# Layer 1's first key, value and query projection taken from the stream before its norm, with the norm applied afterwards

## The chip, the cores and the metric

One core of a Trainium2 chip runs the whole program as one launch. The metric is the device time of that launch in microseconds; the time before is the median of three runs. A profile of one further execution gives the instructions of each engine: TensorE (PE, with its weight loads as PEld), VectorE (DVE), ScalarE (ACT), GpSimd (POOL) and SyncE (SP), whose queue issues the DMAs of this kernel. Times inside the execution are counted from the start of its span.

## What is computed

A backbone of two layers over 512 latent tokens and 256 context tokens of width 2048. The part that matters here is the entry of layer 1, the odd one:

```python
mod = silu_c @ w_mod[l] + b_mod[l]
shift, scale, gate = jnp.split(mod[:, None, :], 3, axis=-1)
...
h = rmsnorm(x, norm_g[l]) * (1.0 + scale) + shift
hc = rmsnorm(cx, norm_g[l]) * (1.0 + cscale) + cshift
...
u = h @ o_w_in[i]
uc = hc @ o_w_in[i]
```

`rmsnorm` divides each token by the root of the mean square over its 2048 values. From `u` come the heads of two attentions (C with 8 query heads on 2 key heads, D with low-rank queries and keys) and a gate. Layer 0 has the same frame with two other attentions.

## The kernel before

All activations lie transposed: 128 channels of the model on the partitions, the 768 tokens (512 latent, 256 context) along the free axis, so the stream is 16 chunks of 128x768. A matrix product of full precision is made of three products in float32r: an operand is split into a high part (ScalarE's cast, `wh`, `h`) and the rest (VectorE's subtraction, `wl`, `l`), and TensorE adds high by high, high by low and low by high (`mm_step`, L277 to L287). Weights come in blocks of 128 output columns; four chunks' worth of a block is one 128x512 tile that is loaded (`wraw`, L274), cast (L265) and subtracted (L224). There are four `wh` and four `wl` buffers and three `wraw` buffers.

Layer 0 ends with 16 output chunks (`out_chunk`, L683). Each adds the gated product to the old stream, stores the new one (`x1d`, L689), squares it on ScalarE (L695) and sums the squares over the chunks on GpSimd (`acc1`, L700), multiplies it on VectorE by `ascale`, which is (1 + scale) times the norm's gain (L697), and stores that to `xad` (L698).

Layer 1 starts at L724. `rstd_cols` (L244) sums the squares over the partitions on TensorE by a product with ones (L249), takes the root on ScalarE (L253) and the reciprocal on VectorE (L254). `spread` (L232) lays the result over all partitions with six small products (L229) and two copies out of PSUM (L236) into the tile `rs1`, 128x768. Then a loop over the 16 chunks k (L731 to L738) loads `xad[k]` (`xk`, L733) and makes the normed input with `make_h` (L351): `xn = xk * rs1` (L353, on VectorE for every third chunk and on GpSimd for the other ten), `h = xn + shift` rounded on ScalarE in two halves (L358), `l = (xn + shift) - h` on VectorE in two halves (L364). The h and l of all 16 chunks stay in 32 buffers, which the products of layer 0's end give free. In the same loop chunk k is multiplied into three accumulators at once (`odd_ps`): the first key block C_K0, the first value block C_V0 (512 latent and 256 context columns each) and the first query block C_Q0 (512 columns). After the loop the key is squared, normed and rotated (L799 to L815), the value is transposed (L816, with L481), the query is treated likewise (L821 to L829), attention starts, and projections of other blocks (`proj`, gates first) fill TensorE meanwhile.

In the background, `mod_later` (L165) computes the modulation for later use: it loads `mraw` (L172) and adds it up in `macc` on VectorE (L179); for layer 1's output gates it is let go only after the last `xk` load (`last_x`).

The order of the work on each engine is set when the program is built, by a scheduler that works on a timeline of its own; the queues then run strictly in that order. That holds for SyncE's queue too: a load that waits for a buffer holds up every DMA behind it.

Of the kernel before, what the change touches and what calls it, by code (L numbers as in the profile page):

```python
# [17 lines left out]
P = 128  # L18
# [23 lines left out]
def trunk_kernel(ctx: ExitStack, tc: tile.TileContext, T):  # L42
# [20 lines left out]
        return pss.tile([P, 1024], F32, tag="S", name="S")  # L63

    def slot(name):
        return sp["s3"].tile([P, TOK], F32, tag="s3", name=name)

    def slotr(name):
        return sp["s3"].tile([P, TOK], F32R, tag="s3", name=name)

    def oslot(name):
        return sp["s3"].tile([P, TOK], F32, tag="o", name=name, bufs=2)
# [156 lines left out]
            nc.tensor.matmul(dst[:, P * i:P * i + P], lhsT=cols[:, 2 * t:2 * t + 1].broadcast_to([P, P]), rhs=ident,  # L229
                             start=True, stop=True)  # L230

    def spread(cols, dst):  # L232
        for ts in ((0, 1, 2, 3), (4, 5)):
            tp = psj.tile([P, 512], F32, name="J")
            spread_to(tp, cols, ts)
            nc.vector.tensor_copy(dst[:, P * ts[0]:P * ts[-1] + P], tp[:, :P * len(ts)])  # L236

# [6 lines left out]
    def rstd_cols(accs, ts, dim, name, bank=jbank):  # L244

        mp = bank()
        steps = [(a, t) for a in accs for t in ts]
        for i, (a, t) in enumerate(steps):
            nc.tensor.matmul(mp[:, 2 * t:2 * t + 2], lhsT=a[:, P * t:P * t + P], rhs=ones[:, 0:2],  # L249
                             start=(i == 0), stop=(i == len(steps) - 1))  # L250
        rs = sm.tile([P, 12], F32, name=name, bufs=2)
        n = 2 * len(ts)
        nc.scalar.activation(rs[:, :n], mp[:, :n], AF.Sqrt, bias=epsc, scale=1.0 / dim)  # L253
        nc.vector.reciprocal(rs[:, :n], rs[:, :n])  # L254
        return rs
# [178 lines left out]
    def etile(name):  # L434
        return sp["ep"].tile([P, TOK], F32, tag="e", name=name)
# [281 lines left out]
    for j in range(NCH):  # L717
# [4 lines left out]


    w = T["ow"]  # L724
    rs1 = etile("rs1")
    spread(rstd_cols((acc1, sq), range(6), D_MODEL, "rsx"), rs1)
    s_start = sbanks()
    odd_cols = (C_K0, C_V0, C_Q0)
    odd_ps = [(psj.tile([P, 512], F32, name="J"), s_start[:, 256 * i:256 * i + 256] if i < 2 else None)
              for i in range(3)]  # L730
    for k in range(NCH):  # L731
        xk = slot("xk")
        last_x = nc.sync.dma_start(xk, xad[k])  # L733
        hT[k] = make_h(1, k, xk, rs1, tmp("xn"), "mod")
        for i, (lat, cx) in enumerate(odd_ps):
            if k % 4 == 0:
                ws4[i] = wsplit(wraw(w, odd_cols[i], k, 4), 4)
            mm_step(lat, cx, ws4[i][k % 4], hT[k], k == 0, k == NCH - 1, opens=(i % 2 == 0), closes=(i % 2 == 1))  # L738

    def scaled(cols, f):  # L740
        nc.vector.tensor_scalar(cols[:, :8], cols[:, :8], f, None, op0=ALU.mult)
# [329 lines left out]
```

## Time and profile before

| | |
|---|---|
| runs before | 2518.85, 2517.13, 2510.58 us; median 2517.13 us |
| the profiled execution | 2515.64 us, of which the span is 2513.9 us |
| mean granted TensorE clock | 0.985 of full speed |
| busy in the span | PE 2408.1 us, DVE 1570.2 us, ACT 1011.7 us, POOL 247.8 us |
| last product of layer 0's output chunks starts | about 1550 us |
| first product of layer 1's loop starts | 1560.08 us |
| last product of that loop starts | 1619.33 us |
| first product of the gate projection behind it | 1628.68 us |

In a row of the timeline the first number is the start, the second the duration; in brackets stands how long the engine sat idle before it and what ended that. An engine's next instruction can start a little before the one ahead is marked as ended, so the distance from start to start is the better price where rows follow closely. In a row of grouped instructions the total and the mean stand behind the bar, then the idle time before them.

### The profile page before, as it was taken

What the parts mean: (1) busy time and instruction counts of PE and PEld (TensorE: products, weight loads), DVE (VectorE), ACT (ScalarE), POOL (GpSimd) and SP (SyncE); (2) the same over time, 40 slices, a digit from 0 to 9 for tenths busy, and PEclk for the clock granted to TensorE, in tenths of its full rate; (3) what the DMA queues carried; (4) which work ended last, traced back from release to release, by engine and by line L of the source; (5) the groups of instructions that cost most, each with busy time, mean ns of one, the idle gap of its engine ahead of it and who ended that gap; (6) DMA issues with size and microseconds to landing.
All of it is one profiled execution on the core that took longest, in us unless ns stands there. A gap on an engine that the chain in (4) does not pass through costs nothing.

```text
span 2513.9 us, 36308 instructions
## 1 busy us (share of the span) xinstructions
PE 2408.1 (96%) x14234; PEld 2077.1 (83%) x14234; DVE 1570.2 (62%) x2796; ACT 1011.7 (40%) x1964; POOL 247.8 (10%) x160
## 2 busy tenths in 40 slices
PE   3898999999999999999989999899999999999998
PEld 1677888888888899989878888688888888888787
DVE  4358667556965787887566664757545336776534
ACT  3234555444454334323342222444434334554434
POOL 1111001001000011010001012200001010100010
PEclk8999999999999999999999999899999999999999
DMA  8853111111312343443325545425422221222234
GB/s 305 302 179 100 43 57 56 50 57 57 109 58 72 100 144 113 142 164 111 134 96 199 188 170 184 146 92 191 150 72 84 69 95 56 64 93 68 97 118 151
DMA packets 97931, 297.48 MB, mean 118 GB/s; under 512 B 11488, under 2 KB 12512, under 8 KB 97760
## 3 DMA queue, kind: packets, MB, share of 16 engines
q1 hardware_dynamic: 97760, 295.16, 34.7%
q8 instruction: 112, 1.84, 0.3%
q14 instruction: 59, 0.48, 0.1%
HBM read 269.16 MB, written 25.95 MB: 117 GB/s over the span
## 4 chain that ended last, share of the span: by engine, by line
PE 87%; DVE 6%; DMA 3%; issue 2%; ACT 1%; SPq 0%; ACTq 0%; DVEq 0%
PE J L284 22%; PE J L287 22%; PE J L285 22%; PE O L563 6%; PE S L505 4%; PE T L548 3%; PE S L501 3%; DMA mraw<-in_wm_dram 2%; PE T L151 1%; DVE macc L179 1%; DVE l L364 1%; PE J L187 1%; DVE wl L224 1%; PE T L249 1%; PE T L229 1%
## 5 line engine op out<-in xcount | busy, mean ns | idle before, releaser
L284 PE MATMUL J<-h,wh 128*128 128x512 f32 (+1 forms) x2224 | 789.0, 356 | 9.3 <-DVE sg L493 3.2
L285 PE MATMUL J<-l,wh 128*128 128x512 f32 (+1 forms) x2224 | 762.5, 353 | 3.6 <-DVE l L364 3.6
L287 PE MATMUL J<-h,wl 128*128 128x512 f32 (+1 forms) x2224 | 704.3, 355 | 9.2 <-DVE wl L224 9.2
L265 ACT CAST wh<-wraw 128x512 fp32r<-128x512 f32 x492 | 304.1, 620 | 682.1 <-PE J L285 581.3
L224 DVE TENSOR_TENSOR wl<-wraw,wh 128x512 fp32r<-128x512 f32 x500 | 363.7, 731 | 317.7 <-ACT wh L265 307.1
L284 PEld LDWEIGHTS J<-h,wh 128*128 128x128 f32 x2224 | 421.3, 189 | 94.3 <-issue 8.2
L285 PEld LDWEIGHTS J<-l,wh 128*128 128x128 f32 x2224 | 421.9, 190 | 56.7 <-DVE l L364 4.8
L287 PEld LDWEIGHTS J<-h,wl 128*128 128x128 f32 x2224 | 386.4, 190 | 44.1 <-DVE wl L224 12.4
L179 DVE SCALAR_TENSOR_TENSOR macc<-mraw,silc,macc 128x512 f32<-128x512 f32 x420 | 317.2, 787 | 34.6 <-DMA mraw<-in_wm_dram 31.9
L284 PE MATMUL J<-yh,wh 128*128 128x512 f32 (+1 forms) x800 | 275.3, 351 | 4.7 <-ACT yh L469 4.7
L285 PE MATMUL J<-yl,wh 128*128 128x512 f32 (+1 forms) x800 | 271.7, 350 | 1.0 <-DVE yl L224 0.9
L287 PE MATMUL J<-yh,wl 128*128 128x512 f32 (+1 forms) x800 | 253.6, 349 | 0.2 <-DVE wl L224 0.2
L517 DVE TENSOR_REDUCE nb<-S 128x1 f32<-128x768 f32 (+3 forms) x208 | 166.2, 799 | 140.0 <-PE S L505 73.0
L552 ACT CAST pth<-T 128x256 fp32r<-128x256 f32 (+2 forms) x288 | 125.0, 450 | 190.4 <-PE T L548 186.6
L284 PEld LDWEIGHTS J<-yh,wh 128*128 128x128 f32 x800 | 149.9, 189 | 31.6 <-ACT yh L469 5.5
L224 DVE TENSOR_TENSOR ptl<-T,pth 128x256 fp32r<-128x256 f32 (+2 forms) x288 | 144.2, 514 | 49.1 <-ACT pth L552 47.3
L285 PEld LDWEIGHTS J<-yl,wh 128*128 128x128 f32 x800 | 150.5, 189 | 22.3 <-DVE yl L224 3.1
L524 ACT ACTIVATE e<-S,nb 128x256 f32<-128x256 f32 (+3 forms) x144 | 104.3, 724 | 156.4 <-DVE nb L517 90.5
L287 PEld LDWEIGHTS J<-yh,wl 128*128 128x128 f32 x800 | 140.4, 189 | 13.2 <-DVE wl L224 0.5
L431 POOL TENSOR_TENSOR r<-r,cos 128x512 f32<-128x512 f32 x31 | 44.3, 1428 | 792.1 <-DVE t L430 736.2
L548 PE MATMUL T<-identr,e 128*128 128x128 f32 x784 | 116.3, 275 | 2.9 <-DVE e L534 2.6
L548 PEld LDWEIGHTS T<-identr,e 128*128 128x128 f32 x784 | 95.2, 142 | 16.7 <-issue 2.8
(283 smaller groups left out, 3143.7 us busy)
## 6 DMA issues: line engine op xcount, KB each, us to landing
mraw<-in_wm_dram SPq DMA_DIRECT2D x128, 512.0 KB, 3.7
wraw<-in_ew_dram SPq DMA_DIRECT2D x102, 512.0 KB, 3.7
wraw<-in_ow_dram SPq DMA_DIRECT2D x64, 512.0 KB, 3.6
wraw<-in_wo_dram SPq DMA_DIRECT2D x62, 512.0 KB, 3.8
mraw<-in_wm_dram SPq DMA_DIRECT2D x80, 384.0 KB, 7.4
xT<-in_xT_dram SPq DMA_DIRECT2D x16, 384.0 KB, 7.6
res<-in_xT_dram SPq DMA_DIRECT2D x16, 384.0 KB, 4.3
xad<-nx SPq DMA_DIRECT2D x16, 384.0 KB, 2.7
```

What stands on the lines that cost most here:

```text
L179: nc.vector.scalar_tensor_tensor(macc[:, v, :], rv[:, i, :], sc, macc[:, v, :], op0=ALU.mult, op1=ALU.add)
L224: nc.vector.tensor_tensor(o, a, h.bitcast(F32), op=ALU.subtract)
L265: nc.scalar.copy(wh[:, :n, :], rv[:, k0:k0 + n, :])
L284: nc.tensor.matmul(o, lhsT=wh, rhs=xh[:, c0:c1], start=first and (opens or o is lat), stop=False)
L285: nc.tensor.matmul(o, lhsT=wh, rhs=xl[:, c0:c1], start=False, stop=False)
L287: nc.tensor.matmul(o, lhsT=wl, rhs=xh[:, c0:c1], start=False, stop=last and (closes or o is lat))
L505: nc.tensor.matmul(S[:, 512:end], lhsT=q, rhs=k[:, 128 * lo:128 * hi], start=(i == 0), stop=(i == n - 1 and not masks))
L517: nc.vector.tensor_reduce(nb, S, axis=AX.X, op=ALU.max, negate=True)
L524: nc.scalar.activation(e, S, AF.Exp, bias=nb, scale=1.0 if scale is None else scale, accum_out=den)
L548: nc.tensor.transpose(out=tp[:, 128 * (b - b0):128 * (b - b0) + 128], in_=e[:, 128 * b:128 * b + 128], identity=ident)
L552: nc.scalar.copy(ph, tv)
L563: nc.tensor.matmul(o, lhsT=v[:, cols[i]], rhs=pt[part][:, i, :], start=(n == 0), stop=(n == len(steps) - 1))
```

## The change

The first loop no longer norms its input. It loads `xad[k]` into a tile of 770 columns, in two DMAs (512 latent columns, 256 context columns), and puts the two shift columns of the chunk (latent and context) between them. It casts and subtracts that tile (`xh`, `xl`, 770 columns wide) and multiplies it into the three blocks, so each accumulator holds the product of the weights with the scaled stream and, in two columns, with the shifts. The latent part takes 512 columns, the part behind it 258; the query block is cut in 256 and 258. `late_norm` then multiplies each accumulator by `rs1` on VectorE and adds the shift's product as a bias on ScalarE, into tiles in SBUF, which the code behind uses in place of the accumulators. `rs1` is now computed behind the loop in the code, with PSUM banks of another pool. A second loop loads every `xad[k]` again, into four buffers (two of tag `o`, two of tag `sg`), norms it in place and makes the h and l of all chunks for the other projections; it makes no product itself. `last_x`, for which the background waits, is now the last load of the first loop.

```diff
     rs1 = etile("rs1")
-    spread(rstd_cols((acc1, sq), range(6), D_MODEL, "rsx"), rs1)
     s_start = sbanks()
     odd_cols = (C_K0, C_V0, C_Q0)
-    odd_ps = [(psj.tile([P, 512], F32, name="J"), s_start[:, 256 * i:256 * i + 256] if i < 2 else None)
-              for i in range(3)]
+    first_ps = [jbank(), pso.tile([P, 512], F32, name="O"), jbank()]
+    q_bank = tbank()
     for k in range(NCH):
-        xk = slot("xk")
-        last_x = nc.sync.dma_start(xk, xad[k])
-        hT[k] = make_h(1, k, xk, rs1, tmp("xn"), "mod")
-        for i, (lat, cx) in enumerate(odd_ps):
+        xk = slot2("xk")
+        last_x = nc.sync.dma_start(xk[:, 0:512], xad[k][:, 0:512])
+        nc.sync.dma_start(xk[:, 514:770], xad[k][:, 512:768])
+        nc.vector.tensor_copy(xk[:, 512:514], modc[1][:, k, :])
+        xh, xl = slot2("xh", F32R), slot2("xl", F32R)
+        nc.scalar.copy(xh, xk)
+        sub(xl, xk, xh)
+        for i in range(3):
             if k % 4 == 0:
                 ws4[i] = wsplit(wraw(w, odd_cols[i], k, 4), 4)
-            mm_step(lat, cx, ws4[i][k % 4], hT[k], k == 0, k == NCH - 1, opens=(i % 2 == 0), closes=(i % 2 == 1))
+            wh, wl = ws4[i][k % 4]
+            if i < 2:
+                regs = ((first_ps[i], 0, 512), (s_start[:, 512 * i:512 * i + 258], 512, 770))
+            else:
+                regs = ((first_ps[i][:, 0:256], 0, 256), (q_bank[:, 0:258], 256, 514))
+            for n, (wk, xx) in enumerate(((wh, xh), (wh, xl), (wl, xh))):
+                for o, c0, c1 in regs:
+                    nc.tensor.matmul(o, lhsT=wk, rhs=xx[:, c0:c1], start=(k == 0 and n == 0),
+                                     stop=(k == NCH - 1 and n == 2))
+    spread(rstd_cols((acc1, sq), range(6), D_MODEL, "rsx", tbank), rs1, tbank)
+
+    def late_norm(name, parts, bias):
+
+        t = slot(name)
+        bc = sm.tile([P, 2], F32, name="bc", bufs=3)
+        nc.vector.tensor_copy(bc, bias)
+        for ps, c0, c1, v in parts:
+            nc.vector.tensor_tensor(t[:, c0:c1], ps, rs1[:, c0:c1], op=ALU.mult)
+            nc.scalar.activation(t[:, c0:c1], t[:, c0:c1], AF.Identity, bias=bc[:, v:v + 1])
+        return t
...
+    for k in range(NCH):
+        xk = (oslot, sgslot)[k % 2]("xk")
+        nc.sync.dma_start(xk, xad[k])
+        hT[k] = make_h(1, k, xk, rs1, xk, "mod")
```

The scheduler places the new instructions as follows. The first place is SyncE's queue where the loop's loads begin; `wraw` are the weights, `xad15` is layer 0's last store. Before:

```order
L274 DMA wraw_14984<-in_ow_dram 128x512
L733 DMA xk_14832<-xad0_109 128x768
L733 DMA xk_14875<-xad1_110 128x768
L689 DMA x1d15_108<-nx_14792 128x512
L733 DMA xk_14900<-xad2_111 128x768
L733 DMA xk_14925<-xad3_112 128x768
L733 DMA xk_14950<-xad4_113 128x768
```

Now, in the same place:

```order
L737 DMA xk_14807<-xad0_109 128x512
L738 DMA xk_14807<-xad0_109 128x256
L692 DMA x1d15_108<-nx_14792 128x512
L277 DMA wraw_15059<-in_ow_dram 128x512
L737 DMA xk_14851<-xad1_110 128x512
L701 DMA xad15_124<-nx_14792 128x768
L738 DMA xk_14851<-xad1_110 128x256
L737 DMA xk_14877<-xad2_111 128x512
L738 DMA xk_14877<-xad2_111 128x256
```

Half of chunk 1's load and all later ones now stand behind the store of `xad15`, which before stood behind the load of chunk 8.

The second place is VectorE's queue around the making of `rs1` (two copies out of PSUM); `xn` and the `xk` of L356 are the normed inputs, `l1_k` the low parts of the second loop, `xl` those of the first. Before:

```order
L254 RECIPROCAL rsx_14815<-rsx_14815 128x12
L697 TENSOR_SCALAR nx_14792<-nx_14792,modc1_194 128x512
L236 COPY rs1_14801<-J_14818 128x512
L236 COPY rs1_14801<-J_14824 128x256
L353 TENSOR_TENSOR xn_14834<-xk_14832,rs1_14801 128x768
L364 SCALAR_TENSOR_TENSOR l1_0_14837<-xn_14834,modc1_194,h1_0_14836 128x512
L364 SCALAR_TENSOR_TENSOR l1_0_14837<-xn_14834,modc1_194,h1_0_14836 128x256
L364 SCALAR_TENSOR_TENSOR l1_1_14880<-xn_14877,modc1_194,h1_1_14879 128x512
```

Now (`xl_14978` is chunk 5's, `xl_15030` chunk 7's):

```order
L227 TENSOR_TENSOR xl_14978<-xk_14973,xh_14977 128x770
L739 COPY xk_14999<-modc1_194 128x2
L227 TENSOR_TENSOR wl_15062<-wraw_15059,wh_15061 128x512
L239 COPY rs1_14801<-T_15311 128x512
L227 TENSOR_TENSOR xl_15004<-xk_14999,xh_15003 128x770
L739 COPY xk_15025<-modc1_194 128x2
L227 TENSOR_TENSOR xl_15030<-xk_15025,xh_15029 128x770
L739 COPY xk_15051<-modc1_194 128x2
L239 COPY rs1_14801<-T_15317 128x256
L356 TENSOR_TENSOR xk_15342<-xk_15342,rs1_14801 128x768
L356 TENSOR_TENSOR xk_15369<-xk_15369,rs1_14801 128x768
L227 TENSOR_TENSOR xl_15056<-xk_15051,xh_15055 128x770
```

The subtractions of chunks 0 to 7 stand ahead of the first normed input. From there on VectorE's queue mixes both loops: the subtraction of chunk 15 stands behind the `l` pair of chunk 14.

The third place is TensorE's queue where the small products of `spread` stand. Before, they are ahead of the loop's first product:

```order
L249 MATMUL J_14802<-ones_189,sq_14796 128x2 x6
L229 MATMUL J_14818<-identr_169,rsx_14815 128x128 x4
L229 MATMUL J_14824<-identr_169,rsx_14815 128x128 x2
L284 MATMUL J_14829<-h1_0_14836,wh_14844 128x512
L284 MATMUL J_14830<-h1_0_14836,wh_14856 128x512
```

Now the second copy's two stand in chunk 6 (`xh_15003`), and the first copy's four are spread over chunk 4:

```order
L753 MATMUL J_14803<-xh_15003,wh_14939 128x512
L753 MATMUL S_14802<-xh_15003,wh_14939 128x258
L753 MATMUL O_14804<-xh_15003,wh_14951 128x512
L753 MATMUL J_14805<-xh_15003,wh_14963 128x256
L753 MATMUL T_14806<-xh_15003,wh_14963 128x258
L232 MATMUL T_15317<-identr_169,rsx_15308 128x128 x2
L753 MATMUL J_14803<-xl_15004,wh_14939 128x512
```

Five chunks of products and the first five of chunk 6 now run ahead of the last small product.

More of the change, by code (lines that the diff above doesn't have):

```diff
@@ L65, in slot, with slot2 @@
     def slot(name):
-        return sp["s3"].tile([P, TOK], F32, tag="s3", name=name)
+        return sp["s3"].tile([P, TOK + 2], F32, tag="s3", name=name)[:, :TOK]
+    def slot2(name, dt=F32):
+        return sp["s3"].tile([P, TOK + 2], dt, tag="s3", name=name)
     def slotr(name):
-        return sp["s3"].tile([P, TOK], F32R, tag="s3", name=name)
+        return sp["s3"].tile([P, TOK + 2], F32R, tag="s3", name=name)[:, :TOK]
     def oslot(name):
@@ L230, in spread_to, with spread @@
                              start=True, stop=True)
-    def spread(cols, dst):
+    def spread(cols, dst, bank=None):
         for ts in ((0, 1, 2, 3), (4, 5)):
-            tp = psj.tile([P, 512], F32, name="J")
+            tp = (bank or jbank)()
             spread_to(tp, cols, ts)
@@ new lines, in trunk_kernel @@
+    spread(rstd_cols((acc1, sq), range(6), D_MODEL, "rsx", tbank), rs1, tbank)
[7 more added lines that the diff above has]
+        return t
+    odd_ps = []
+    for i in range(2):
+        cx = s_start[:, 512 * i:512 * i + 258]
+        t = late_norm("first", ((first_ps[i], 0, 512, 0), (cx[:, 2:258], 512, 768, 1)), cx[:, 0:2])
+        odd_ps.append((t[:, :512], t[:, 512:768]))
@@ L740, in scaled @@
+    t = late_norm("first", ((first_ps[2][:, 0:256], 0, 256, 0), (q_bank[:, 0:256], 256, 512, 0)), q_bank[:, 256:258])
+    odd_ps.append((t[:, :512], None))
+    for k in range(NCH):
+        xk = (oslot, sgslot)[k % 2]("xk")
+        nc.sync.dma_start(xk, xad[k])
+        hT[k] = make_h(1, k, xk, rs1, xk, "mod")
     def scaled(cols, f):
```

## The prediction

> **What bounds the kernel now.** I read the page first, then the busy time of the stretches around the change, then the groups and the timeline of the engine that is full there.
>
> ```profile
> span 2513.9 us, 36308 instructions
> ```
>
> The stretches (busy time of PE, PEld, DVE, ACT, POOL with counts, then clock, DMA share, GB/s) are cut at the start of the loop's first product, at the last `l`, at the loop's last product and at the first gate product:
>
> ```profile
> 1550.70:1560.08 9.38, 5.62 (x36) 5.16 (x35) 4.62 (x10) 2.15 (x5) 1.64 (x1) 0.82 0.96 318
> 1560.08:1602.94 42.86, 36.11 (x156) 28.27 (x157) 42.79 (x48) 20.78 (x38) 20.88 (x10) 0.84 0.47 169
> 1602.94:1619.56 16.62, 15.80 (x85) 13.27 (x85) 9.02 (x14) 4.52 (x9) 0.00 (x0) 1.00 0.83 259
> 1619.56:1628.68 9.12, 6.30 (x39) 5.73 (x38) 5.05 (x9) 3.27 (x9) 1.79 (x2) 0.81 0.54 181
> 1628.68:1700.00 71.32, 71.32 (x357) 60.46 (x358) 41.76 (x76) 33.30 (x58) 8.31 (x6) 0.98 0.26 90
> ```
>
> While the normed inputs are made, VectorE is busy 42.79 of 42.86 us: it sets the pace, not TensorE. Then TensorE catches up for 16.62 us, waits around the key's norm for 9.12 us, and is full afterwards. So what is lost before 1628.68 is lost for good. What VectorE did in its full stretch, by form:
>
> ```profile
> L364 DVE SCALAR_TENSOR_TENSOR l<-xn,modc,h 128x256 fp32r<-128x256 f32 x16 | 18.6, 1166 | 0.0
> L364 DVE SCALAR_TENSOR_TENSOR l<-xn,modc,h 128x512 fp32r<-128x512 f32 x16 | 15.7, 980 | 0.8 <-ACT h L358 0.8
> L353 DVE TENSOR_TENSOR xn<-xk,rs 128x768 f32<-128x768 f32 x5 | 4.7, 949 | 0.1
> L224 DVE TENSOR_TENSOR wl<-wraw,wh 128x512 fp32r<-128x512 f32 x6 | 4.0, 676 | 0.0
> L179 DVE SCALAR_TENSOR_TENSOR macc<-mraw,silc,macc 128x512 f32<-128x512 f32 x5 | 3.7, 738 | 0.0
> ```
>
> The narrow half of `l` takes longer than the wide one, which it should not. The timeline of VectorE at its undisturbed end gives the true prices, from start to start:
>
> ```profile
> 1596.95 0.94 DVE L353 TENSOR_TENSOR xn<-xk,rs 128x768 f32<-128x768 f32 x1
> 1597.82 0.47 DVE L364 SCALAR_TENSOR_TENSOR l<-xn,modc,h 128x256 fp32r<-128x256 f32 x1
> ...
> 1598.87 1.13 DVE L364 SCALAR_TENSOR_TENSOR l<-xn,modc,h 128x512 fp32r<-128x512 f32 x2
> 1599.93 1.28 DVE L224 TENSOR_TENSOR wl<-wraw,wh 128x512 fp32r<-128x512 f32 x2
> 1601.14 0.74 DVE L179 SCALAR_TENSOR_TENSOR macc<-mraw,silc,macc 128x512 f32<-128x512 f32 x1
> 1601.80 1.13 DVE L364 SCALAR_TENSOR_TENSOR l<-xn,modc,h 128x512 fp32r<-128x512 f32 x2
> ```
>
> An `xn` of 768 columns costs 0.87, an `l` pair 1.06, a `wl` 0.60, a `macc` step 0.66. By these, the stretch should hold 16 x 1.06 + 5 x 0.87 + 6 x 0.60 + 5 x 0.66 = 28.2 us; it took 42.8. The other 14.6 us are the ten norms on GpSimd, 1.46 each: a GpSimd row, then the VectorE row that began behind it.
>
> ```profile
> 1582.84 2.15 POOL L353 TENSOR_TENSOR xn<-xk,rs 128x768 f32<-128x768 f32 x1 [0.41 <-DVE l L364]
> ```
>
> ```profile
> 1583.23 2.69 DVE L364 SCALAR_TENSOR_TENSOR l<-xn,modc,h 128x512 fp32r<-128x512 f32 x2
> ```
>
> The pair took 2.69 instead of 1.13 us, since VectorE stood until GpSimd was done. The Trainium skill has the rule in "SBUF — State Buffer", section "Who interferes with whom": a VectorE instruction with two inputs in SBUF and a GpSimd one that reads SBUF shut each other out, and the second to come waits out the first. The trace agrees, with 2.69 us against 1.13.
>
> **The change, part by part.**
>
> *TensorE's work stays.* At full clock (a product's start, then the next block's):
>
> ```profile
> 1617.80 0.40 PE L284 MATMUL J<-h,wh 128*128 128x512 f32 x1
> ...
> 1618.85 0.40 PE L284 MATMUL J<-h,wh 128*128 128x512 f32 x1
> ...
> 1619.56 1.40 PE L249 MATMUL T<-ones,sq 128*128 128x2 f32 x12
> 1622.19 2.57 PE L229 MATMUL T<-identr,rsx 128*128 128x128 f32 x12 [1.23 <-DVE rsx L254]
> 1624.56 1.49 PE L481 MATMUL J<-identr,ev 128*128 128x128 f32 x6
> ...
> 1628.68 0.50 PE L284 MATMUL J<-h,wh 128*128 128x512 f32 x1 [0.84 <-ACT ev L825]
> ```
>
> A key or value step (2304 columns) takes 1.05 us, so 2.19 columns a nanosecond, and a query step 0.71. The two or three added columns and the cut query block change nothing by this rate: 2.81 us a chunk, 45 for all.
>
> *The start moves little.* ScalarE's queue has chunk 0's cast behind layer 0's last square:
>
> ```profile
> 1550.34 0.62 ACT L265 CAST wh<-wraw 128x512 fp32r<-128x512 f32 x1 [3.59 <-PE J L285]
> 1551.81 0.84 ACT L695 ACTIVATE sq<-nx 128x768 f32<-128x768 f32 x1 [0.85 <-DVE nx L688]
> ```
>
> With 0.9 for 770 columns (0.62 for 512) chunk 0 starts about 1553.5, without the norm. Chunk 1 cannot follow so soon.
>
> ```profile
> 1554.69 0.41 DVE L697 TENSOR_SCALAR nx<-nx,modc 128x512 f32<-128x512 f32 x1
> ```
>
> ```profile
> 1555.51 0.60 SPq L698 DMA_DIRECT2D xad<-nx  x1
> ```
>
> ```profile
> DMA to landing us min/median/max: 3.8/5.4/8.3
> ```
>
> Half of its load stands behind the store of `xad15`, which waits for that VectorE row. Even if the store goes 0.8 us sooner (the reciprocal no longer stands ahead), that half is issued about 1555 and lands at 1559 to 1560.5; with the cast, chunk 1 starts at about 1560, where before the whole loop started. The gain here is chunk 0's 2.8 us, and it only makes TensorE wait earlier.
>
> *`rs1` comes late.* Before, its second copy was here:
>
> ```profile
> 1557.79 0.42 DVE L236 COPY rs<-J 128x256 f32<-128x256 f32 x1 [0.16 <-PE J L229]
> ```
>
> that is, ready at 1558.2. Now its small products stand in chunks 4 and 6 of TensorE's queue. From 1560: five chunks, 14.05; five products of chunk 6 (1796 columns), 0.8; the small products at the row's 2.57; a cold clock at the start, 1.3 (below); the copy, 0.4. That makes 1579.1. VectorE has nothing to do in between but eight `xl` and three `wl`, as its queue stops at the copies. The 20.9 us before the first normed input are the core of my forecast.
>
> ```profile
> 1562.57 0.63 PE L285 MATMUL J<-l,wh 128*128 128x512 f32 x1
> 1562.99 0.63 PE L287 MATMUL J<-h,wl 128*128 128x512 f32 x1
> ```
>
> The cold clock: these wide products are 0.42 us apart, against 0.23 at full clock, for some 3 us after the idle start. The Trainium skill states in "TensorE: Matmul & The Clock Gate", section "What's actually happening", that an idle window of about 3.4 us halves the clock until a busy one has passed. By that the charge, as an estimate, would be 1.7 us in place of 1.3.
>
> *VectorE from `rs1` to the end of the first loop.* Its queue then holds, up to the `xl` of chunk 15: 15 `l` pairs (15.9), 6 `xn` (5.2), 8 `xl` (768 wide and two inputs like `xn`, so 0.87 each, 7.0), 6 `wl` (3.6), 7 copies of two columns (0.7 at 0.1 each, an estimate below every row here). Sum 32.4 us. The `xl` are new work, the `macc` steps are gone from here. GpSimd still does its ten norms, and the new `xl` have two SBUF inputs as well, so they wait too: 14.6 us as before at most, 0 if every norm falls into a wait. I take 12, close to the measured end, since the queue has little idle time once `rs1` is there. If VectorE lost each norm's whole 2.15 us, it would be 21.5. Behind the last `xl` TensorE has 13 products, 4370 columns, 2.0 us. So the loop ends at 1579.1 + 32.4 + 12 + 2.0 = 1625.5, against 1619.56: **+5.9** (-6.1 with no blocking, +8.5 with 14.6).
>
> *The tail.* Before, the squares could read the accumulators, and 6.5 us after the loop's end the transposes (L481) were done, 9.12 us after it the gate started. Now VectorE first multiplies by `rs1` (four pieces for key and value, with a `macc` and a `wl` between them) and ScalarE adds the bias:
>
> ```profile
> 1623.95 0.69 DVE L813 TENSOR_TENSOR ev<-ev,T 128x512 f32<-128x512 f32 x1 [1.81 <-PE T L229]
> 1624.80 0.42 DVE L813 TENSOR_TENSOR ev<-ev,T 128x256 f32<-128x256 f32 x1 [0.17 <-PE T L229]
> ```
>
> Two of each, 2.2, with 0.66 and 0.60 between makes 3.5; about 1.3 of it runs while the value and query steps finish. ScalarE then has the bias of the last piece, the squares and a scaled copy ahead of the column sums, at its rows about 2 us more:
>
> ```profile
> 1619.23 0.38 ACT L802 ACTIVATE sq<-S 128x256 f32<-128x256 f32 x1
> 1619.50 0.47 ACT L806 ACTIVATE ev<-S,vcol 128x256 f32<-128x256 f32 x1
> ```
>
> So the transposes end about 10.8 us after the loop (6.5 + 3.5 - 1.3 + 2), the gate follows at once, and the query's column sums come among its products (0.8): 11.6 against 9.1, **+2.5** (0 to +4).
>
> *Moved work.* The 15 `macc` steps go from the loop to behind it:
>
> ```profile
> L179 DVE SCALAR_TENSOR_TENSOR macc<-mraw,silc,macc 128x512 f32<-128x512 f32 x15 | 11.2, 745 | 7.6 <-DMA mraw<-in_wm_dram 7.4
> ```
>
> VectorE has room there (41.76 of 71.32 us busy), but its queue is in order: a `macc` that waits for its load holds up the key's and query's norm and the gates' `wl` behind it. 7.6 us of such waits stood before; TensorE has projections for cover. **+1** (0 to +7.6).
>
> *At nothing:* the second loads of chunks 0 to 3 stand among layer 0's output loads, a chunk behind the stores they need, so SyncE has no wait there; should the queue stop for a store's landing, each would cost at most the 5.4 us of a load, and three weight buffers cover it. The other loads (16 tiles of 128x768 floats, 6.3 MB) run while DMAs are at half their time (0.47 in the full stretch).
>
> Sum: 5.9 + 2.5 + 1 = +9.4. On the profiled execution's 2515.64 us that is 2525.0; the median of the runs is 1.5 above, so **2526** for the median. With the blocking between 10 and 14.6, the forecast's own range is 2523 to 2532.
>
> **The rivals.**
>
> - *TensorE sets the pace (faster).* If `rs1` and the l's don't hold the first loop, as the change in words says, it ends at 1560 + 15 x 2.81 + 1.3 + 2.6 = 1606: -13.5, with tail and moved work -10, a median of 2507. It needs the `xl` to overtake the `l` pairs; VectorE's queue has them behind. For it: the loop before waited for the normed inputs, which now nobody needs in it. Chance 0.14.
> - *No blocking (same).* GpSimd's norms fall into VectorE's waits for the second loads, which have only four buffers. Then the loop ends at 1613.5: -6.1 + 3.5 = -2.6, 2514.5. Against it: 14.6 us lost in the present loop. With half the blocking, +4.7. Chance 0.34 for this and what lies up to +7.5.
> - *The ring of four buffers decides (slower still).* A second load waits for the `l` of four chunks earlier: load 5.4, GpSimd 2.15, ScalarE 1.1 (row below), `l` 1.06, and 1.5 (an estimate: four issues at about 0.4, seven took 3.70) in SyncE's queue, where the first loop's loads stand between: 11.2 a round. The first four end about 12 us after `rs1`, three more rounds 34: 1625, and `xl` 15 and its products 3 us later, if SyncE's stops add 5 more: 1633, +13.5 + 3.5 = +17, 2534. It decides where a round is longer than VectorE's own 4 chunks, 11.1 us by my sum ((32.4 + 12) / 4). Chance 0.18.
>
> ```profile
> 1559.30 1.12 ACT L358 ACTIVATE h<-xn,modc 128x512 fp32r<-128x512 f32 x2 [4.79 <-DVE xn L353]
> ```
>
> ```profile
> 1551.71 3.70 SPq L733 DMA_DIRECT2D xk<-xad  x7
> ```
>
> The forecast itself has 0.34.
>
> **How the numbers follow.** A measurement of this kernel can tell about 0.3%, 7.6 us, from no change. Forecast and third rival lie above it (the forecast barely): slower 0.34 + 0.18 = 0.52; the second lies within it: same 0.34; the first: faster 0.14. The range goes from the first rival's 2507 to 2538, the third's 2534 with the 4 us that tail and moved work may add. The change not doing what it says is no case: the loop's products do start without `rs1`.
>
> **What would show it.** Right: chunk 1's first product near 1560; the second copy of `rs1` near 1579; VectorE nearly full from there to the last `xl`, with `l` and `xl` rows of 2 us beside GpSimd's; the loop's last product near 1625 and the gate's first near 1637. Wrong: a second copy of `rs1` before 1570, or a loop that ends before 1615. Should the loop end on time and the loss come later, the moved `macc` steps are the place to look.

## The result, and the profile after

Four runs of the changed kernel took 2529.87 to 2532.85 us, median 2531.23; the kernel before now has four runs with a median of 2515.07. The ratio is 1.0065, with a 95% interval of 1.0046 to 1.0085: slower by 16 us. The forecast was 2526, with a range to 2538. The profiled execution took 2531.32 us, its span 2529.5, which is 15.6 more than the span before.

The same five stretches as before, cut at the loop's first product, the end of `rs1`, the last `xl`, the loop's last product and the gate's first (busy time of PE, PEld, DVE, ACT, POOL with counts, then clock, DMA share, GB/s):

```profile
1554.14:1581.81 27.67, 27.67 (x166) 25.57 (x166) 11.81 (x24) 7.88 (x12) 0.00 (x0) 0.88 0.56 180
1581.81:1629.95 48.14, 33.31 (x144) 27.96 (x143) 47.35 (x58) 26.75 (x46) 22.55 (x10) 0.75 0.66 213
1629.95:1632.64 2.69, 2.69 (x18) 2.25 (x16) 2.69 (x6) 2.26 (x5) 0.00 (x0) 1.00 0.03 6
1632.64:1643.57 10.93, 5.90 (x31) 5.85 (x31) 9.15 (x20) 6.33 (x14) 0.00 (x0) 0.73 0.69 244
1643.57:1700.00 56.43, 56.14 (x278) 46.81 (x277) 40.70 (x64) 24.73 (x45) 8.87 (x6) 0.99 0.36 116
```

TensorE is full for 27.67 us, with the products of the first seven chunks and the small ones of `rs1`. Then it is the other way round: for 48.14 us VectorE is full (47.35 busy) and TensorE waits a third of the time. The loop ends at 1632.64, 13.1 after the old 1619.56; the gate starts 14.9 after the old 1628.68; from there to the end of the span it is 885.9 us against 885.2. So the loss is in the loop, and the rest is small. (Layer 0 ended 0.65 us later in this execution, which is in the 13.1.)

How `rs1` came, from TensorE, ScalarE, SyncE and VectorE in one place:

```profile
1578.76 0.61 PE L232 MATMUL T<-identr,rsx 128*128 128x128 f32 x4
```

```profile
1574.51 0.43 SPq L738 DMA_DIRECT2D xk<-xad  x1
```

```profile
1579.48 0.84 ACT L741 CAST xh<-xk 128x770 fp32r<-128x770 f32 x1 [3.04 <-DMA xk<-xad]
```

```profile
1580.41 0.96 DVE L227 TENSOR_TENSOR xl<-xk,xh 128x770 fp32r<-128x770 f32 x1 [2.90 <-ACT xh L741]
1581.36 0.42 DVE L239 COPY rs<-T 128x256 f32<-128x256 f32 x1
1581.81 3.49 DVE L356 TENSOR_TENSOR xk<-xk,rs 128x768 f32<-128x768 f32 x2
1585.22 2.56 DVE L227 TENSOR_TENSOR xl<-xk,xh 128x770 fp32r<-128x770 f32 x1
```

The small products were done at 1579.4, but the copy has the `xl` of chunk 7 ahead of it in VectorE's queue, and that waited for its load, issued at 1574.5 and landed five microseconds later. So the copy ended at 1581.8, not at 1579.1. Behind it the first GpSimd norms start, and the `xl` that follows takes 2.56 us instead of 0.96.

What VectorE did in the full stretch, by form (total, mean ns, then idle time):

```profile
L367 DVE SCALAR_TENSOR_TENSOR l<-xk,modc,h 128x512 fp32r<-128x512 f32 x16 | 15.7, 982 | 0.8 <-ACT h L361 0.8
L367 DVE SCALAR_TENSOR_TENSOR l<-xk,modc,h 128x256 fp32r<-128x256 f32 x15 | 14.9, 995 | 0.0
L227 DVE TENSOR_TENSOR xl<-xk,xh 128x770 fp32r<-128x770 f32 x9 | 10.2, 1128 | 2.9 <-ACT xh L741 2.9
L356 DVE TENSOR_TENSOR xk<-xk,rs 128x768 f32<-128x768 f32 x6 | 7.3, 1225 | 0.0
```

The narrow `l` again costs more than the wide one, and now the `xl` and `xn` rows are too long as well. By the prediction's prices the work up to the last `xl` is 32.4 us. Of the 48.14, 0.8 is idle (the 2.9 and one of the nine `xl` lie ahead of the copy, and the last wide `l` only begins in the stretch). What is left, 15.0 us, is as much as 1.5 for each of the ten GpSimd norms that ran beside it, as before. That GpSimd is the cause is what e2 and e6 test.

The end of the loop and its tail on TensorE, and the last loads in SyncE's queue:

```profile
1632.36 0.28 PE L753 MATMUL T<-xh,wl 128*128 128x258 f32 x1
```

```profile
1636.95 2.07 PE L252 MATMUL T<-ones,sq 128*128 128x2 f32 x12 [4.31 <-ACT sq L841]
1639.73 2.90 PE L232 MATMUL T<-identr,rsx 128*128 128x128 f32 x12 [0.71 <-DVE rsx L257]
1642.43 1.49 PE L484 MATMUL J<-identr,ev 128*128 128x128 f32 x6
1643.57 0.78 PE L287 MATMUL J<-h,wh 128*128 128x512 f32 x1
```

```profile
1621.59 0.32 SPq L777 DMA_DIRECT2D xk<-xad  x1
1621.96 0.42 SPq L737 DMA_DIRECT2D xk<-xad  x1
```

```profile
1627.74 0.84 ACT L741 CAST xh<-xk 128x770 fp32r<-128x770 f32 x1 [2.37 <-DMA xk<-xad]
1629.00 0.95 DVE L227 TENSOR_TENSOR xl<-xk,xh 128x770 fp32r<-128x770 f32 x1
```

The tail is 10.93 us, of which 4.31 is the wait for the late norm and its squares. The second set of rows raised a question that the prediction had weighed only in its third rival, with 5 us: the first loop's last load (L737) stands in SyncE's queue behind the last second load (L777), which waits for a buffer, so for an `l`. In the stretch from 1575 to 1636 SyncE waited 29.7 us for `l` in that way:

```profile
SPq L777 <- DVE l L367: 29.7, 12, 10.6
SPq L277 <- DVE wl L227: 3.1, 5, 1.4
```

### The profile page after: what moved, and what is told of

Its sections match the earlier page's. It is cut to its first block, busy times and chain, and to the rows that moved or that the text cites. A ratio compares the mean times of both kernels' runs of the same rounds, so it can differ in the third digit from the quotient of the medians.

```text
span 2529.5 us, 36538 instructions
## 1 busy us (share of the span) xinstructions
PE 2413.1 (95%) x14282; PEld 2083.7 (82%) x14282; DVE 1594.7 (63%) x2837; ACT 1027.6 (41%) x1986; POOL 248.1 (10%) x160
## 4 chain that ended last, share of the span: by engine, by line
PE 86%; DVE 6%; DMA 5%; issue 2%; ACT 1%; SPq 0%; ACTq 0%; DVEq 0%
PE J L287 21%; PE J L290 21%; PE J L288 21%; PE O L566 6%; PE S L508 4%; DMA mraw<-in_wm_dram 3%; PE T L551 3%; PE S L504 3%; DVE macc L182 1%; PE T L154 1%; DVE wl L227 1%; PE T L252 1%; PE J L190 1%; DVE l L367 1%; DMA xT<-in_xT_dram 1%
## 5 line engine op out<-in xcount | busy, mean ns | idle before, releaser
L287 PE MATMUL J<-h,wh 128*128 128x512 f32 (+1 forms) x2176 | 769.1, 355 | 4.5 <-DVE sg L496 3.2
L288 PE MATMUL J<-l,wh 128*128 128x512 f32 (+1 forms) x2176 | 741.0, 351 | 0.0
L290 PE MATMUL J<-h,wl 128*128 128x512 f32 (+1 forms) x2176 | 682.3, 352 | 7.3 <-DVE wl L227 7.3
L227 DVE TENSOR_TENSOR wl<-wraw,wh 128x512 fp32r<-128x512 f32 x500 | 366.3, 736 | 321.2 <-ACT wh L268 309.7
L287 PEld LDWEIGHTS J<-h,wh 128*128 128x128 f32 x2176 | 411.3, 189 | 86.8 <-issue 8.4
L288 PEld LDWEIGHTS J<-l,wh 128*128 128x128 f32 x2176 | 411.5, 189 | 50.9
L290 PEld LDWEIGHTS J<-h,wl 128*128 128x128 f32 x2176 | 376.3, 190 | 39.4 <-DVE wl L227 8.8
L227 DVE TENSOR_TENSOR ptl<-T,pth 128x256 fp32r<-128x256 f32 (+2 forms) x288 | 144.3, 514 | 51.3 <-ACT pth L555 49.8
```

The lines of the kernel that those rows point to most:

```text
L227: nc.vector.tensor_tensor(o, a, h.bitcast(F32), op=ALU.subtract)
L287: nc.tensor.matmul(o, lhsT=wh, rhs=xh[:, c0:c1], start=first and (opens or o is lat), stop=False)
L288: nc.tensor.matmul(o, lhsT=wh, rhs=xl[:, c0:c1], start=False, stop=False)
L290: nc.tensor.matmul(o, lhsT=wl, rhs=xh[:, c0:c1], start=False, stop=last and (closes or o is lat))
```

## The experiments

Theory A was the prediction's: VectorE's queue from a late `rs1` on, with the `xl`, the `l` and the stops behind GpSimd in it, sets the end of the loop. The rivals: the ring of four buffers (the prediction's third), the queue of SyncE that couples both loops, and the moved `macc` steps. The columns of the table behind the second are taken from the profiled execution of each kernel and count, in us, from the start of layer 0's last output row on VectorE (L690; 1550.57 before, 1551.22 after, 1547.99 to 1553.12 in the others), since layer 0 ends at slightly different times. "Against before" is the difference of the medians on the same chip, then the ratio with its interval. The intervals reach some 2 to 5 us to each side, so two rows of the table that differ by less than about 5 us (6 against the changed kernel) do not tell their kernels apart.

| kernel | against before | `rs1` | last `xl` | last `l` | loop's last product | gate starts |
|---|---|---|---|---|---|---|
| before | | 7.6 | | 52.4 | 69.0 | 78.1 |
| changed | +16.2; 1.0065 [1.0046, 1.0085] | 30.6 | 78.7 | 79.8 | 81.4 | 92.4 |
| e1 `rs1` early | +23.2; 1.0095 [1.0081, 1.0109] | 10.3 | 80.6 | 61.4 | 83.6 | 96.2 |
| e2 norms on VectorE | +16.3; 1.0059 [1.0045, 1.0072] | 30.6 | 68.9 | 81.3 | 71.2 | 86.1 |
| e4 `macc` later | +20.0; 1.0081 [1.0067, 1.0095] | 32.4 | 81.6 | 82.6 | 83.9 | 94.5 |
| e7 seven buffers | +30.8; 1.0121 [1.0107, 1.0135] | 22.2 | 86.0 | 67.5 | 90.4 | 103.0 |
| e3 second loop held back | +21.7; 1.0079 [1.0064, 1.0093] | 30.5 | 62.3 | 128.8 | 65.3 | 90.0 |
| e6 before, norms on VectorE | -5.6; 0.9969 [0.9957, 0.9982] | 7.6 | | 47.8 | 58.1 | 71.6 |
| e8 second loads by GpSimd | +24.9; 1.0095 [1.0081, 1.0110] | 32.2 | 83.4 | 85.9 | 87.5 | 98.3 |
| e10 e1 + e2 + e8 | +8.8; 1.0030 [1.0021, 1.0039] | 10.5 | 70.3 | 58.0 | 73.4 | 84.7 |
| e11 weights apart | +22.7; 1.0095 [1.0081, 1.0109] | 34.4 | 83.4 | 86.8 | 87.5 | 97.7 |
| e12 e10 + weights apart | +7.1; 1.0032 [1.0020, 1.0043] | 12.1 | 68.6 | 58.9 | 73.5 | 84.7 |
| e15 e12 with late `rs1` | +15.6; 1.0068 [1.0054, 1.0081] | 35.1 | 74.0 | 88.2 | 76.3 | 92.4 |
| e14 e3 + weights apart | +20.2; 1.0078 [1.0065, 1.0092] | 35.1 | 57.2 | 124.9 | 61.8 | 85.1 |

### GpSimd's norms: e2 and e6

The same edit, in the changed kernel (e2) and in the kernel before (e6). Layer 0 keeps its norms as they were.

```diff
-        (nc.gpsimd if k % 3 else nc.vector).tensor_tensor(xn, xk, rs, op=ALU.mult)
+        (nc.gpsimd if k % 3 and l == 0 else nc.vector).tensor_tensor(xn, xk, rs, op=ALU.mult)
```

> The changed kernel with all 16 norms of the second loop on VectorE and none on GpSimd. My theory (each GpSimd norm costs VectorE 1.5 us of standing still, more than the 0.87 us of doing it itself): 10 x 0.87 = 8.7 us more work, 15.0 us less standing, loop end near 1626, 6.3 less than the changed kernel's +16.2, so +10 against the kernel before (+8 to +12); no two-input row of VectorE beyond 1.2 us in that stretch. Rival, the long VectorE rows have another cause (its share of SBUF taken by the DMAs, say) and GpSimd is a real help: 8.7 more, +25. Rival, the ring of four buffers sets the pace: the norm in a round gets 1.3 us shorter, four rounds, so about -5 as well, but with VectorE idle by several us between the rows; the idle time tells these apart.

> The kernel before the change with all 16 norms of layer 1 on VectorE. If the 14.6 us that VectorE loses to ten GpSimd norms are real and its queue sets the pace there, its full stretch is 14.6 - 8.7 = 5.9 us shorter: 5.9 less than the kernel before (-4 to -6.5). Rival, from the same edit in the changed kernel, where the loop ended sooner but nearly nothing was left of it at the end: the steps behind (the key's norm, the first scores) take most of it back, -1.

The rows of e2 between 1581 and 1630, then those of e6 between 1560 and 1602, have their plain lengths again (mean ns behind the total):

```profile
L356 DVE TENSOR_TENSOR xk<-xk,rs 128x768 f32<-128x768 f32 x16 | 15.0, 953 | 1.1 <-DMA xk<-xad 0.9
L367 DVE SCALAR_TENSOR_TENSOR l<-xk,modc,h 128x256 fp32r<-128x256 f32 x14 | 6.7, 476 | 0.0
```

```profile
L353 DVE TENSOR_TENSOR xn<-xk,rs 128x768 f32<-128x768 f32 x16 | 15.1, 954 | 0.1
L364 DVE SCALAR_TENSOR_TENSOR l<-xn,modc,h 128x256 fp32r<-128x256 f32 x16 | 7.7, 481 | 0.0
```

In e6 the narrow `l` fell from 1166 ns to 481, the stretch from `rs1` to the last `l` from 44.7 to 40.2 us, and the kernel became 5.6 us faster than the one before (-5.9 expected). That is the best version of this study. So the stops behind GpSimd are real, and ten norms cost VectorE more by waiting than by doing them. They are not why the change is slower: with all norms on VectorE on both sides it costs 21.9 us (+16.3 and -5.6), not less than 16.2. In e2 the loop ended 10.2 us sooner than in the changed kernel (6.3 expected; the new order also has four `l` behind the last `xl` in place of one), the gate 6.2, but at the end nothing to speak of was left. The last `l`, which the gate needs, is no sooner (81.3 against 79.8), and the next chain came up at once: TensorE ran out of gate work and waited for the query. From the gate to 1750 the same 555 products took 4.5 us longer than in the changed kernel, with 3.7 us idle in place of 0.3, and the products right behind the wait ran 0.43 us apart in place of 0.23.

```profile
1653.68 0.58 PE L504 MATMUL S<-kh,qh 128*128 128x256 f32 x1 [2.14 <-ACT qh L472]
```

### The late rs1, alone: e1

```diff
     rs1 = etile("rs1")
+    spread(rstd_cols((acc1, sq), range(6), D_MODEL, "rsx", tbank), rs1, tbank)
     s_start = sbanks()
...
-    spread(rstd_cols((acc1, sq), range(6), D_MODEL, "rsx", tbank), rs1, tbank)
```

> The changed kernel with one line moved back: rs1 is computed ahead of the first loop in the program, as before the change. My theory (VectorE's queue from rs1 to the last xl sets the end of the loop, and rs1 came 20 us late): the second copy of rs1 is done near 1561 in place of 1581.8; behind it VectorE has 14 xl (12.3 us), 14 copies (1.0), 16 l pairs (17.0), 6 xn (5.2), 9 wl (5.4) and the 15.0 us that it stood behind GpSimd, 55.9 us in all, so its last xl ends near 1617 and the loop near 1620 in place of 1632.6: 12.7 us less than the changed kernel's +16.2, that is +3.5 against the kernel before (+0.5 to +6.5). Rival, the ring of four buffers sets the pace: its rounds start 20 us earlier too and the loop ends near 1613, so -4. Rival, the lateness of rs1 is covered by first-loop products that TensorE can make meanwhile: no change, +16.

None of the three came true: the kernel got 7 us slower than the changed one, a little more than the noise between the two. `rs1` was ready 20 us sooner and the last `l` came 18 us sooner, as theory A has it, but the last `xl` came 2 us later. The order on each queue is made anew with the edit, and now the second loop runs ahead, and the first loop's last loads wait. SyncE, ScalarE and VectorE of e1 at that place:

```profile
1608.81 0.42 SPq L739 DMA_DIRECT2D xk<-xad  x1
1619.46 0.33 SPq L277 DMA_DIRECT2D wraw<-in_ow_dram  x1
1619.89 0.38 SPq L738 DMA_DIRECT2D xk<-xad  x1
```

```profile
1618.09 0.62 ACT L268 CAST wh<-wraw 128x512 fp32r<-128x512 f32 x1 [4.61 <-PE S L754]
```

```profile
1618.74 0.69 DVE L227 TENSOR_TENSOR wl<-wraw,wh 128x512 fp32r<-128x512 f32 x1 [4.19 <-ACT wh L268]
```

SyncE stands for 10 us on the load of a gate weight. That load waits for a `wraw` buffer, the buffer for a `wl` (L227), the `wl` for a `wh`, and the `wh` for TensorE to be done with the block's weights of the four chunks before. The next `xk` of the first loop stands behind it. Once the last `l` is made, VectorE is busy only 7.0 of the 19.2 us up to the last `xl`. In the trace of e1 SyncE waits 17.3 us for `wl` between 1575 and 1636 (3.1 in the changed kernel):

```profile
SPq L277 <- DVE wl L227: 17.3, 7, 10.1
```

### The ring of buffers, and SyncE's queue: e7 and e8

```diff
-        xk = (oslot, sgslot)[k % 2]("xk")
+        xk = (oslot, sgslot, tmp, oslot, sgslot, tmp, tmp)[k % 7]("xk")
```

> The changed kernel with seven buffers in place of four for the second loads (three more of the pool of temporary tiles, which the loop leaves unused). My theory (VectorE's work sets the pace, with only 0.8 us idle in 48 us): no change beyond 1.5 us, +16 against the kernel before (+14.5 to +18). Rival, the ring of four buffers set the loop's end, which came at 1632.6, close to the 1633 of that rival in the prediction: with seven buffers the loop ends where VectorE alone would, near 1625, so +8.5.

```diff
-        nc.sync.dma_start(xk, xad[k])
+        nc.gpsimd.dma_start(xk, xad[k])
         hT[k] = make_h(1, k, xk, rs1, xk, "mod")
```

> The changed kernel with the second loads issued from GpSimd's queue in place of SyncE's, nothing else changed in the text. Theory A (VectorE's full queue sets the loop's end, SyncE's order does not matter): the same work in nearly the same order, the last xl one or two l pairs sooner, +14 to +16 against the kernel before. Theory B (the first loop's last loads stand in SyncE's queue behind second loads that wait for an l, so both queues turn in step): without that wait xk 15 is loaded several us sooner, ScalarE's casts no longer wait for loads (17.6 us of such waits between 1550 and 1650 now), VectorE may show idle time, and the loop ends 5 us or more sooner: +11 or below. Rival: GpSimd's own queue now holds its norms behind loads that wait, and VectorE starves: slower than +17.

Seven buffers made it 14.6 us slower still, though `rs1` came 8.4 us sooner in the new order. The second loop ran ahead (last `l` at 67.5), VectorE then was idle more than half of the time, and the last two loads of the first loop again came behind gate weights. VectorE of e7:

```profile
1634.15 0.96 DVE L227 TENSOR_TENSOR xl<-xk,xh 128x770 fp32r<-128x770 f32 x1 [6.79 <-ACT xh L741]
```

So the rival of the ring falls as it was put: with more buffers the loop did not end where VectorE alone would. Theory A's "no change" falls as well. In e1 and e7 alike the second loop ended sooner than in the changed kernel (its last `l` by 18.4 and 12.3 us) and the first one later (its last `xl` by 1.9 and 7.3). e8 freed SyncE's queue of the second loads and lost 8.7 us against the changed kernel, as its last rival said: now a norm stands in GpSimd's queue behind loads that wait for an `l`, and then waits for its own load. GpSimd of e8, and the busy times of that stretch, with VectorE (third) no longer full:

```profile
1624.14 0.55 POOL L777 DMA_DIRECT2D xk<-xad  x1 [1.19 <-DVE l L367]
1625.20 0.54 POOL L777 DMA_DIRECT2D xk<-xad  x1 [0.51 <-issue]
1628.61 3.80 POOL L356 TENSOR_TENSOR xk<-xk,rs 128x768 f32<-128x768 f32 x2 [2.87 <-DMA xk<-xad]
```

```profile
1620.00:1630.00 10.00, 7.43 (x30) 6.40 (x31) 8.38 (x11) 2.98 (x5) 5.41 (x6) 0.67 0.94 356
```

### The moved macc steps: e4

The loads of the last four blocks now wait for the first head's gate store; the number of ticks is the same.

```diff
-            tick(3.5)
+            if h:
+                tick(3.5)
             finish(1, h, o, sg, 512)
-            tick(3.5)
+            if h:
+                tick(3.5)
...
-            nc.sync.dma_start(sgd[h], sg[:, :512])
+            st = nc.sync.dma_start(sgd[h], sg[:, :512])
+            if h == 0:
+                last_x = st
+                tick(7)
```

> The changed kernel with the macc steps of layer 1's output gates released later: their loads wait for the first head's store of its gate, and the background is ticked for that head only behind it. No macc row then stands between the loop and the first gates. My theory (the moved steps cost little, two of 0.66 us in the chain from the loop's end to the gate): -1.3 against the changed kernel, so +15 against the kernel before (+13 to +16.5). Rival, the moved steps and their waits for loads are what the tail costs: at least 4 us less, +12 or below.

Both missed: +20.0 lies outside either range. The 3.8 us above the changed kernel are within the noise, but no gain is there. No `macc` row stands in the tail any more, and from the loop's end to the gate it took 10.6 us in place of 10.9, so the steps cost that tail about 0.3 us. The loop itself ended 2.5 us later, with `rs1` 1.8 later, which this edit does not explain by itself; the order was made anew here too. At their new place TensorE was busy 47.52 of the 50 us from 1700 on, against 50.00 in the changed kernel.

```profile
1700.00:1750.00 50.00, 47.52 (x248) 40.19 (x247) 34.63 (x62) 21.36 (x38) 4.64 (x4) 0.97 0.57 187
```

### The first loop by itself: e3, e14 and e11

In e3 the second loop norms with a copy of `rs1` that is made behind the last `xl`:

```diff
+    rs2 = etile("rs2")
+    nc.vector.tensor_copy(rs2[:, 0:1], xl[:, 0:1].bitcast(F32))
+    nc.vector.tensor_copy(rs2, rs1)
     for k in range(NCH):
...
-        hT[k] = make_h(1, k, xk, rs1, xk, "mod")
+        hT[k] = make_h(1, k, xk, rs2, xk, "mod")
```

> The changed kernel with the second loop held back: it norms with a copy of rs1 that is made only after the last xl of the first loop, so VectorE's queue has all 16 xl ahead of the first norm. Theory 1 (VectorE's work up to the last l is the bound, whatever its order): the first loop ends near 1607, 25 us sooner, but the 16 l pairs, 6 xn and the standing behind GpSimd now begin there and take 45 to 50 us beside the late norm and the key's steps, so the last l comes near 1655 instead of 1631, and the gate, which needs them one by one, starts soon and crawls: +20 against the kernel before (+16 to +26). Theory 2 (what counts is that the first loop ends early, as in the first rival of the prediction): +2 or below. Theory 3 (the first loop is held by its own loads and weights, as the two experiments with an early rs1 and with seven buffers suggest): it ends well behind 1607 even with nothing of the second loop ahead of it.

e11 is the changed kernel, e14 is e3, each with this:

```diff
-                ws4[i] = wsplit(wraw(w, odd_cols[i], k, 4), 4)
+                ws4[i] = wsplit(wraw(w, odd_cols[i], k, 4, tmp("wr")), 4)
```

> The kernel with the second loop held back (+21.7 us), with the raw weights of the first loop in tiles of their own. There the first loop ran alone and still ended at 1615.0, not near 1606. Theory C (SyncE's queue: loads of the stream behind weight loads that wait for a buffer): it now ends near 1608 (1606 to 1611), since no load of it waits behind a gate weight; the total stays high, +18 (+15 to +22), as VectorE's second loop begins only there. Rival D (the four buffers of split weights hold it): no change, 1615.

> The changed kernel with one edit: the first loop's raw weights are loaded into the three temporary tiles, so that loads of gate weights no longer wait in SyncE's queue for the first loop's weight buffers. Theory A (in the changed kernel as it is, the last loads of the first loop follow second loads that wait for an l, and VectorE makes these without a pause; the gate weights are not what holds it): the loop ends within 1.5 us of where it does now, +16 against the kernel before (+14 to +18). Theory C (the gate weights ahead of the last two loads hold the loop in the changed kernel too): 4 us less or more than that, +12 or below.

With nothing of the second loop ahead of it, the first loop still ended at 65.3, only 3.7 us before the old loop, which made the h and l besides. TensorE had 45 us of products there, by the prediction's 2.81 a chunk. VectorE waited for casts, these for loads, and SyncE, with the loads, for `wl` (the first two rows from 1556 to 1625, the third from 1575 to 1636):

```profile
DVE xl L227 <- ACT xh L741: 26.5, 12, 6.0
ACT xh L741 <- DMA xk<-xad: 26.5, 7, 6.2
SPq L277 <- DVE wl L227: 25.4, 6, 10.3
```

So theory 3 held for the loop's end, and theory 1 for the total: +21.7, +20 expected. The last `l` came at 128.8, that is at 1678, as VectorE had the whole second loop still to do; theory 1 had put it at 1655. In e14 the loop ended 3.5 us sooner than in e3, half of what theory C expected. Part of the rest is a side effect: the first weights were now loaded only at 1552.24, in SyncE's queue behind the store of layer 0's last output (1551.82), and TensorE waited for them at the start. That the temporary tiles were not free sooner is likely, but not shown.

```profile
1557.82 0.79 PE L753 MATMUL J<-xh,wh 128*128 128x512 f32 x1 [6.70 <-ACT wh L268]
```

The same late start is in e11 (its first product comes at 1557.07, `rs1` 3.8 us later than in the changed kernel by the table), so its +6.5 against the changed kernel tells no size, and a gain of the 4 us of theory C could be hidden behind that start. What speaks against theory C in the changed kernel is its own trace, in which SyncE waited only 3.1 us for `wl`, 1.4 at most at a time.

### All obstacles away: e10, e12 and e15

e10 has the edits of e1, e2 and e8 together, e12 the weights apart besides, and e15 is e12 without the edit of e1.

> Three edits together on the changed kernel: rs1 early, all norms on VectorE, the second loads from GpSimd's queue. Theory A (VectorE alone): from rs1 at 1561 the 41 us of its own work and ten more norms (8.7) end at 1611, loop end near 1614, gate near 1625, 18 us sooner than now: -2 against the kernel before. Theory C (the early-rs1 run showed that two loads of the first loop stand in SyncE's queue behind a gate weight that waits for a weight buffer, which waits in turn for chunk 11's products; from chunk 11's xl to the loop's end it took 22 us there): xl 11 comes near 1602, the loop ends near 1624, the gate starts near 1635, +8 (+5 to +11).

> The kernel of the three edits (rs1 early, all norms on VectorE, second loads from GpSimd's queue; +8.8 us) and the raw weights of the first loop in tiles of their own. Theory C: the two loads that stood behind a gate weight until 1611 there now come in time, and VectorE alone sets the pace: from rs1 at 1560.7 some 50 us of work and 2.5 of waits, last xl near 1613.5 in place of 1620.5, loop end near 1616.5, gate near 1628, about 7 less: +1 against the kernel before (-2 to +4). Rival D, the four buffers of split weights and TensorE's own waits at each fourth chunk hold the first loop anyway: loop end near 1621, +6 or more.

> The same with rs1 late again, as in the changed kernel. It tells what the lateness of rs1 costs once loads and GpSimd are out of the way. By the prediction's own reading (the 20 us ahead of the first normed input are the core) the loop ends 12 us or more later than with rs1 early: +13 against the kernel before. By VectorE's queue as it now stands (its last xl is ahead of the last four l pairs and three norms): behind rs1 at 1581.8 it has about 41 us up to the last xl less 7, 1616, so the loop ends at most 3 us later and only the last l, near 1627, is late: +4 (+1 to +7). Rival, lateness costs nothing: the same as with rs1 early.

e10 came at +8.8 with its gate at 1634.89, as theory C had said, and not at theory A's -2. The profiled execution of e10 is among its shorter runs (2520.5 against a median of 2524.8), so its times serve for the place, not for the sum. e12 took only 1.7 us less, which is within the noise and nearer to rival D's figure, but not for its reason: no gate weight stands ahead of the first loop's last loads any more and the last `xl` came 1.7 us sooner, yet the loop ended no sooner (73.5 against 73.4). With loads and casts there, what is left is the order on VectorE: all 16 `l` are made before the last five `xl`, and TensorE, which waited 10.1 us for `xl` in the course of the loop, has five chunks to catch up on at the end (5 x 2.81 = 14 us, from the `xl` at 1608.3 to the loop's end at 1622.9). VectorE of e12, and the waits of its TensorE from 1555 to 1625:

```profile
1605.11 3.26 DVE L367 SCALAR_TENSOR_TENSOR l<-xk,modc,h 128x512 fp32r<-128x512 f32 x6
1608.28 0.95 DVE L227 TENSOR_TENSOR xl<-xk,xh 128x770 fp32r<-128x770 f32 x1
```

```profile
PE J L754 <- DVE xl L227: 10.1, 9, 2.1
PE J L754 <- ACT wh L268: 2.5, 1, 2.5
```

e12 is also the fairest match to e6, the kernel before with its norms on VectorE: between the two lie 12.7 us (+7.1 and -5.6). That is near the 14 us that 16 `xl` at 0.87 add to VectorE's queue, but as e12 moves loads and weights too, this cause is argued, not shown.

e15 against e12 is the price of the late `rs1` by itself in that surrounding: 8.5 us in the medians, more than the noise, between the 3 and the 12 that were expected. The loop ends 2.9 us later, as VectorE's queue said, and the other part is in the tail, where the last norms and `l` stand among the pieces of the late norm: 16.0 us from the loop's end to the gate, against 11.3.

## Why the prediction was right, and where its steps failed

The sign, the place and the engine were right: slower, nearly all of it in the loop, with VectorE full behind a late `rs1`. The sum was 6 us short in the profiled execution: +9.4 against +15.7 (2531.32 - 2515.64).

- *Chunk 1 at 1560.* It was 1562.85, though its cast was done at 1559.74. TensorE's queue had the column sums of `rs1` between chunk 0's first products and its others, and these others then ran 0.43 us apart, at a granted clock of 0.51 (1558.97 to 1562.71). They took 3.7 us, 1.7 more than at the full rate, where the sum had charged 1.3. TensorE around there:

```profile
1555.08 1.90 PE L252 MATMUL T<-ones,acc 128*128 128x2 f32 x12
1556.84 2.27 PE L252 MATMUL T<-ones,sq 128*128 128x2 f32 x10
...
1561.26 0.63 PE L753 MATMUL O<-xh,wl 128*128 128x512 f32 x1
1561.69 0.42 PE L753 MATMUL S<-xh,wl 128*128 128x258 f32 x1
...
1562.85 0.48 PE L753 MATMUL J<-xh,wh 128*128 128x512 f32 x1
```

- *`rs1` at 1579.1.* The copy ended at 1581.8. This step named TensorE's small products as the last to come. They ended at 1579.37, against 1578.7 in the sum, but that is partly luck: chunk 1 was 1.5 us late, with the sum's 1.3 for the cold clock counted in; the products up to the last small ones took 15.9 in place of 14.85; and those small ones took 0.6 in place of 2.57. The copy then stood behind an `xl` that waited for its load, which the sum did not have. Of the 2.7 us, 0.65 is the later end of layer 0.
- *VectorE from `rs1` to the last `xl`, 32.4 + 12.* It took 48.1: the work as summed, 0.8 idle, and 15.0 behind GpSimd. Here the step that chose 12, below the 14.6 measured before, was the mis-sized term. The measured end of that range was right, at 1.5 us for each norm, and e2 and e6, where the rows have their plain lengths without GpSimd, show it to be GpSimd's.
- *The products behind the last `xl`:* 2.7 in place of 2.0. With these three the loop ends 7.1 us after the forecast's 1625.5.
- *The tail, +2.5:* measured +1.8. *The moved `macc` steps, +1:* from the gate on the span is 0.7 longer. e4 shows that they are not what the tail costs.
- *"The 20.9 us before the first normed input are the core."* This holds in part only. An early `rs1` alone gained nothing (e1, +7), and with the second loads, the first loop's weights and GpSimd's norms out of the way it was worth 8.5 us (e12 and e15), not some 20.
- *The rival in which TensorE sets the pace (2507)* came about in no run: even with nothing of the second loop ahead of it on VectorE the first loop took until 61.8 to 65.3 (e14, e3), not the 55.4 of that rival (1606), and the price was the second loop's VectorE work behind it. Weight loads that wait in SyncE's in-order queue held it in part (25.4 us of such waits in e3, 3.5 us gained with weights apart in e14); the prediction did not weigh them. What held the rest is not shown.
- *The rival without blocking* is ruled out by the 15.0 us; *the ring of four buffers* came nearest, with 1633 for the loop's end and 2534 for the time. Its mechanism is not what the trace shows: a ring that sets the pace leaves VectorE waiting, and that was 0.8 us of 48.14; and more buffers did not move the loop's end towards VectorE's own time (e7). So its near figure is luck, as far as these runs show.

What stays open: in the changed kernel VectorE is full and SyncE's queue turns in step with it, and no run here separates the two without making a new order on all queues. That VectorE's work counts is shown by e2, whose loop ended 10 us sooner, though some 3 of these are three more `l` pairs that its order puts behind the last `xl`; that SyncE's order alone would have held the loop as long is not shown.

## What to carry to other kernels

When the input of a product is made a second time, the new work lands on the engine that split it the first time; where that engine already set the pace, moving the norm behind the product did not win in any order tried here (+7.1 at best), whatever TensorE no longer waited for. Two loops that share one in-order load queue and one weight ring can delay each other: letting the second start earlier, or giving it more buffers, took time from the first here. An edit that makes a new order on every queue does not test one cause alone, so its trace has to say what else moved. And where VectorE is full, a norm handed to GpSimd can cost VectorE more (1.5 us each here) than doing it itself (0.87).

## What the runs showed of the hardware

A copy of two columns stood behind GpSimd too. VectorE of e1, with the GpSimd norm beside it:

```profile
1588.20 1.80 DVE L740 COPY xk<-modc 128x2 f32<-128x2 f32 x1
```

```profile
1587.65 2.33 POOL L356 TENSOR_TENSOR xk<-xk,rs 128x768 f32<-128x768 f32 x1 [7.78 <-DMA xk<-xad]
```

It took 1.80 us in place of 0.15, and ended with the norm at 1589.98. In e4, e8 and e11 seven more such copies took 1.79 to 2.07 us and ended with a GpSimd norm in the same way. Of four that by their rows had begun just ahead of a norm, three (in the changed kernel, e1 and e11) took 0.15 to 0.16 and one (in e8) 2.07. It has one input, so the rule of two inputs that the prediction drew on does not cover it. The Trainium skill does, in "SBUF — State Buffer", section "Who interferes with whom": copies between SBUF tiles can run in a mode that takes the shared ports as well, and the trace agrees, with 1.80 against 0.15.
